# Sums of x1's halves on VectorE, and the low half of a half tile behind the next addition: a hybrid decoder layer on one core

## The chip, the cores and the metric

One core of a Trainium2 chip. The metric is device microseconds of one execution of the whole layer; less is better. The kernel before takes 2071.34 us (median of three runs, 2071.24 to 2073.43).

## The reference

One decoder layer in float32 on 512 tokens of width 2048. A token mixer (a gated recurrence and differential attention) and its output projection come first; then a residual and a layer norm; then a gated MLP of width 5632 with a causal convolution of width 3 behind the up-projection; then a residual and a second layer norm. Cut to the part that matters here:

```python
mix = jnp.einsum('bsm,md->bsd', jnp.concatenate([rg_out, at_out], axis=-1), w_out[i])
x = _layernorm(DEEPNORM_ALPHA * x + mix, ln_mix_g[i], ln_mix_b[i])
hu = _causal_dwconv(jnp.einsum('bsd,df->bsf', x, w_up[i]), ffn_conv_w[i], ffn_conv_b[i])
g, u = jnp.split(hu, 2, axis=-1)
ffn = jnp.einsum('bsf,fd->bsd', jax.nn.gelu(g) * u, w_down[i])
```

The x of the second line is called x1 here.

## The kernel before

Every matmul is made of several in a rounded format: a value is split into a high half (ScalarE copies it, rounded, L113) and a low half (VectorE subtracts the high half from the value, L114), and a product takes high x high, high x low and low x high (`mm3`, L120). So a matrix operand is ready for TensorE only when ScalarE and then VectorE have been over it.

Tokens are cut into 4 tiles of 128 (`QB`), the width of 2048 into 16 tiles of 128 (`KT`) or 4 blocks of 512 (`NF`). The stages around the change are these.

**The norms.** The last part of the output projection runs over 4 token tiles and, in each, over 4 blocks `fb` (L722 to L735). For each block TensorE makes six matmuls, VectorE adds them onto y and sums the row (`RowNorm.add`, L585), and ScalarE squares the result with its row sum (L592). Behind the four blocks come the mean (L597 to L600), the variance and its root (L604 to L608) and, in `norm_z`, the scaling of y: block 0 on ScalarE (L711), block 1 on VectorE, the others on GpSimd, except that block 2 of the last token tile is VectorE's too (L714). Each scaled block is stored (L715).

**x1, turned.** `turn_x1` (L666) makes half a tile of x1 with the width on the partitions and 256 tokens along the row: TensorE transposes two blocks (L672), ScalarE scales and shifts them into `x1f` (L682) and copies the high half, VectorE makes the low half (`split`, L684). There are 32 such half tiles, in the order of the list `first`; the first seven hold only tokens of the first two token tiles, which are scaled already while the last token tile is added up. Three of them (`LEAD`) are turned ahead, in the last token tile before blocks 1, 2 and 3 (L725). After that the loop at L739 turns half tile i + 3 and then multiplies half tile i with weights into four sums (`up_first`, L686, 12 matmuls each).

All this, from L721 to L742, is under `tc.manual_schedule()`: each engine gets its instructions in the order in which they are written. Behind that section, a planner orders each engine's instructions by their priority (the place in the program) and by the times at which its own model takes their inputs to be ready. Each engine then works through its queue in that order.

**Two plain blocks.** The results of the first two up-projections are activated (`activate`, four `tap`s on ScalarE, L778, convolutions on VectorE, L772). Then two more blocks of the up-projection run plainly (the loop `for i in range(2, PLAIN)`), in eight units of 48 matmuls. After each unit `forms(j)` (L749) makes the operands of the stage after: of x1f[j] and x1f[j + 8], each in two halves of 256 tokens, four sums are formed (L755 to L758, on GpSimd) into two temporary tiles from a ring of 12, and each sum is split into a high and a low half (L764, L765 and the helper's L113, L114). The weights of each unit are split as well (`wlo<-raw,whi` is their low half).

**The stage after.** 40 blocks of the up-projection use seven products of half size each in place of eight, on the operands that `forms` made. For these, GpSimd's queue issues DMAs that add one block of weights onto another in place (`onto`, L804).

Of the kernel before, what the change touches and what calls it, by code (L numbers as in the profile page):

```python
# [12 lines left out]
AF = mybir.ActivationFunctionType  # L13
ALU = mybir.AluOpType
# [10 lines left out]
QB = S // P  # L25
# [35 lines left out]
LEAD = 3  # L61
# [13 lines left out]
def f32(ap):  # L75
    return ap.bitcast(F32)
# [3 lines left out]
def trunk_kernel(  # L80
    ctx, tc, xT, x_tok, w_qkg, w_v, gate_w, w_out, w_up0, w_up, w_down, ln1, ln2, consts, out
):
    nc = tc.nc
# [10 lines left out]
    def bank():  # L94
        return psum.tile([P, S], F32, tag="ps", bufs=8, name="ps")

    def a_tile(dt=F32R, name="a"):
        return act.tile([P, S], dt, tag="a", bufs=A_BUFS, name=name)

    def t_tile(dt=F32, name="t"):  # L100
        return tmp.tile([P, S], dt, tag="t", bufs=T_BUFS, name=name)

    def c_tile(name):
        return W.pool.tile([P, 2 * S], F32, tag="c", bufs=4, name=name)
# [4 lines left out]
    def split(src, hi=None, lo=None, mk=a_tile):  # L109

        hi = mk(F32R, "hi") if hi is None else hi
        lo = mk(F32R, "lo") if lo is None else lo
        nc.scalar.activation(hi, src, AF.Copy)  # L113
        nc.vector.tensor_tensor(lo, src, f32(hi), ALU.subtract)  # L114
        return hi, lo

    def mm3(ps, w, x, first, last, onto=False):

        for n, (a, b) in enumerate(((w[0], x[0]), (w[0], x[1]), (w[1], x[0]))):
            nc.tensor.matmul(  # L120
                ps, a, b, start=first and n == 0, stop=last and n == 2, skip_group_check=onto
            )
# [85 lines left out]
    def col(i, n=1):  # L208
        return cst[:, i : i + n]
# [410 lines left out]
    def token(tt):  # L620
        return slice(tt * P, (tt + 1) * P)

    for fb in range(NF):
# [7 lines left out]
        for u in range(UO):  # L631
# [7 lines left out]
            for n in range(2):  # L639
                i = 2 * u + n  # L640
# [7 lines left out]
        for tt in range(QB):  # L648
            y = ys[tt, fb] = a_tile(F32, "y")
# [4 lines left out]
    x1 = [[None, None] for _ in range(KT)]  # L654
# [5 lines left out]
    def sides(z):  # L660
        return z[:, :HALF], z[:, HALF:]

    def split2(z):
        return z[:, :S], z[:, S:]

    def turn_x1(n, h):  # L666

        kt, tok = ks[n], halves[h]
        pt = bank()[:, :HALF]
        for i in range(2):  # L670
            c = slice(kt % 4 * P, (kt % 4 + 1) * P)
            nc.tensor.transpose(pt[:, i * P : (i + 1) * P], ys[2 * h + i, kt // 4][:, c], ident)  # L672
        if h == 0:
            j = kt % (KT // 2)
            if j < 4:

                if kt == j:
                    x1f[kt], x1f[kt + KT // 2] = split2(c_tile("x1f"))
            else:
                x1f[kt] = a_tile(F32, "x1f")  # L680
        y = x1f[kt][:, tok]
        nc.scalar.activation(y, pt, AF.Identity, scale=col(C_G1 + kt), bias=col(C_B1 + kt))  # L682
        x1[kt][h] = a_tile(F32R, "x1")
        split(y, *sides(x1[kt][h]))  # L684

    def up_first(n, h):  # L686
        kt, tok = ks[n], halves[h]
        if wu[n] is None:
            wu[n : n + 2] = W.take()
        hi, lo = wu[n]  # L690
        for t in range(4):
            c = slice(t * P, (t + 1) * P)
            mm3(
                pu[t][:, tok], (hi[:, c], lo[:, c]), sides(x1[kt][h]),
                n + h == 0, n == KT - 1 and h == 1,
            )

    first = [
        (n - h * AHEAD, h) for n in range(KT + AHEAD) for h in range(2) if n - h * AHEAD in range(KT)
    ]  # L700
    def norm_root(tt):
        norms[tt].var()

    def norm_z(tt):

        nmean, r = norms[tt].nmean, norms[tt].rstd()
        nc.vector.tensor_tensor(norms[tt].d2, nmean, r, ALU.mult)
        for fb in range(NF):
            y = ys[tt, fb]
            if fb == 0:  # L710
                nc.scalar.activation(y, y, AF.Identity, scale=r, bias=norms[tt].d2)  # L711
            else:
                eng = nc.vector if fb == 1 or (fb == 2 and tt == QB - 1) else nc.gpsimd
                eng.tensor_scalar(y, y, nmean, r, ALU.add, ALU.mult)  # L714
            nc.sync.dma_start(x1d[tt][:, fb * S : (fb + 1) * S], y)  # L715
# [5 lines left out]
    with tc.manual_schedule():  # L721
        for tt in range(QB):  # L722
            norms.append(RowNorm())
            for fb in range(NF):
                if tt == QB - 1 and 0 < fb <= LEAD:  # L725
                    turn_x1(*first[fb - 1])
                ps = bank()
                for n in range(2):
                    hs = [z[:, token(tt)] for z in ms[2 * UO + n]]
                    mm3(ps, hs, wl[fb][n], n == 0, n == 1)  # L730
                norms[tt].add(fb, ys[tt, fb], ps)

                if tt and fb < 2:
                    (norm_root, norm_z)[fb](tt - 1)
            norms[tt].mean()  # L735
        norm_root(QB - 1)
        norm_z(QB - 1)
        pu = [bank() for _ in range(4)]
        for i, at in enumerate(first):  # L739
            if i + LEAD < len(first):  # L740
                turn_x1(*first[i + LEAD])
            up_first(*at)  # L742


# [3 lines left out]

    def forms(j):  # L749
        a, b = x1f[j], x1f[j + KT // 2]  # L750
        sub = nc.gpsimd.tensor_tensor
        t14, t23 = t_tile(F32, "t14"), t_tile(F32, "t23")
        (t1, t4), (t2, t3) = sides(t14), sides(t23)
        (b11, b12), (b21, b22) = sides(a), sides(b)
        sub(t1, b12, b11, ALU.subtract)  # L755
        sub(t2, t1, b22, ALU.subtract)
        sub(t4, t2, b21, ALU.add)
        sub(t3, b22, b12, ALU.subtract)  # L758
        form["p1", j], form["p2", j] = x1[j][0], x1[j + KT // 2][0]
        form["p3", j] = x1[j + KT // 2][1]  # L760
        for name, t in (("p5", t1), ("p4", t4)):
            z = form[name, j] = a_tile(F32R, "hl")
            hi, lo = sides(z)
            nc.scalar.activation(hi, t, AF.Copy, scale=-1.0)  # L764
            nc.vector.scalar_tensor_tensor(lo, t, -1.0, f32(hi), ALU.mult, ALU.subtract)  # L765
        for name, t in (("p6", t2), ("p7", t3)):
            form[name, j] = a_tile(F32R, "hl")
            split(t, *sides(form[name, j]))
# [147 lines left out]
    for i in range(2, PLAIN):  # L916
        pss = []
        for g in range(2):
            ps = bank()
            for half in range(2):  # L920
                parts = W.take()
                left = 4 * (PLAIN - i) - 2 * g - half
                if left <= 6:
                    step(-left, "before", -6, 5)
                for kk in range(8):
                    kt = half * 8 + kk
                    hi, lo = parts[kk // 4]
                    c = slice((kk % 4) * P, (kk % 4 + 1) * P)
                    for h, tok in enumerate(halves):
                        mm3(  # L930
                            ps[:, tok], (hi[:, c], lo[:, c]), sides(x1[kt][h]),
                            kt + h == 0, kt == KT - 1 and h == 1,
                        )
                forms(j)
                j += 1
            pss.append(ps)
        activate(i, pss)
# [36 lines left out]
    for c, n in enumerate(CHUNKS[:-1]):  # L974
        ready(at + n)
        for fb in range(NF):
            ps = [bank() for _ in range(QB)]
            if c == 0:
# [4 lines left out]
                for tt in range(QB):  # L983
                    y = acc[tt, fb] = a_tile(F32, "acc")
# [14 lines left out]
            for tt in range(QB):  # L999
                y = acc[tt, fb]  # L1000
# [102 lines left out]
def build(arrays):  # L1103
    import concourse.bacc as bacc

    nc = bacc.Bacc("TRN2", target_bir_lowering=False, num_devices=1)
    args = [
        nc.dram_tensor(f"in_{n}", arrays[n].shape, F32, kind="ExternalInput").ap() for n in _INS
    ]
    args.append(nc.dram_tensor("out", (S, D), F32, kind="ExternalOutput").ap())  # L1110
    with tile.TileContext(nc) as tc:
        trunk_kernel(tc, *args)
    return nc
# [10 lines left out]
```

## Time and profile before

| | |
|---|---|
| median of the runs | 2071.34 us (2071.24 to 2073.43) |
| the profiled execution, its own time | 2071.46 us |
| its span, from the first instruction to the last | 2069.6 us |
| TensorE busy | 2043.6 us (99%) |
| VectorE busy | 1377.7 us (67%) |
| ScalarE busy | 1038.2 us (50%) |
| GpSimd busy | 135.0 us (7%) |
| mean granted clock of TensorE | 0.995 of full speed |

A busy TensorE says little of what limits it, since its matmuls follow each other closely all the way. What counts is where it is not busy, what ended each such wait, and where its clock was granted at half. In rows, PE is TensorE, PEld its weight load, DVE VectorE, ACT ScalarE, POOL GpSimd. Times are in us from the start of the span; a row of the timeline may hold several instructions in succession (x2).

### The profile page before, as it was taken

The numbers are of one execution on the slowest core, as the hardware profiler recorded it, in microseconds if no ns is written. First come the engines' busy times: TensorE is split into PE (matmuls) and PEld (weight loads), VectorE is DVE, ScalarE is ACT, GpSimd is POOL, SyncE is SP. The second block draws the span as 40 slices with busy tenths as digits, with TensorE's granted clock in tenths as the row PEclk, the third lists the DMA queues.
The fourth block names the chain that finished last, engine by engine and source line by source line (L and its number), as shares of the span: only waits on it lengthen the run. The fifth ranks groups of instructions, "written<-read, shape, count | busy, mean of one in ns | idle before, by whom it ended". The sixth has DMA issues, their size and how long they took to land.

```text
span 2069.6 us, 27751 instructions
## 1 busy us (share of the span) xinstructions
PE 2043.6 (99%) x10535; PEld 1749.7 (85%) x10535; DVE 1377.7 (67%) x2116; ACT 1038.2 (50%) x1652; POOL 135.0 (7%) x193
## 2 busy tenths in 40 slices
PE   9999999999999989999999999999999999999997
PEld 7888888888888889888888888888888888888886
DVE  6566645778335587888888888888889643333346
ACT  5475735668223745565566566565566232222232
POOL 1000000000000150001000000100000000000000
PEclk9999999999999999999999999999999999999999
DMA  6223222223522425576676676676678843243322
GB/s 221 97 72 97 75 96 79 87 82 113 183 92 102 157 73 128 158 191 171 166 190 173 164 187 178 164 185 176 169 182 272 278 138 117 92 142 92 112 82 82
DMA packets 93157, 290.53 MB, mean 140 GB/s; under 512 B 10336, under 2 KB 10336, under 8 KB 93024
## 3 DMA queue, kind: packets, MB, share of 16 engines
q1 hardware_dynamic: 81504, 246.81, 35.7%
q0 software_dynamic: 11520, 41.95, 11.8%
q8 instruction: 83, 1.36, 0.3%
q14 instruction: 50, 0.41, 0.1%
HBM read 268.80 MB, written 19.92 MB: 140 GB/s over the span
## 4 chain that ended last, share of the span: by engine, by line
PE 94%; ACT 3%; DVE 2%; issue 0%; DMA 0%; DVEq 0%
PE ps L120 55%; PE ps L134 37%; DVE x L114 1%; PE ps L364 1%; ACT gt L473 0%; PE ps L365 0%; ACT s L376 0%; PE ps L394 0%; PE ps L672 0%; ACT a L479 0%; ACT L491 0%; ACT L479 0%; ACT L473 0%; ACT L376 0%; DVE hh L495 0%
## 5 line engine op out<-in xcount | busy, mean ns | idle before, releaser
L114 DVE TENSOR_TENSOR wlo<-raw,whi 128x512 fp32r<-128x512 f32 (+1 forms) x672 | 601.2, 913 | 421.4 <-ACT whi L113 420.1
L113 ACT ACTIVATE whi<-raw 128x512 fp32r<-128x512 f32 (+1 forms) x672 | 522.6, 802 | 471.8 <-PE ps L120 412.1
L120 PE MATMUL ps<-wlo,hi 128*128 128x512 f32 x992 | 386.3, 389 | 0.6 <-DVE wlo L114 0.6
L120 PE MATMUL ps<-whi,hi 128*128 128x512 f32 x992 | 385.9, 389 | 0.4 <-ACT hi L113 0.4
L120 PE MATMUL ps<-whi,lo 128*128 128x512 f32 x992 | 385.8, 389 | 0.0
L134 PE MATMUL ps<-hl,whi 128*128 128x512 f32 x1280 | 320.5, 392 | 0.0
L134 PEld LDWEIGHTS ps<-hl,whi 128*128 128x128 f32 x1280 | 230.2, 189 | 41.1
L134 PE MATMUL ps<-x,whi 128*128 128x512 f32 x960 | 237.1, 389 | 0.0
L120 PEld LDWEIGHTS ps<-wlo,hi 128*128 128x128 f32 x992 | 186.3, 188 | 39.7 <-DVE wlo L114 1.2
L120 PEld LDWEIGHTS ps<-whi,hi 128*128 128x128 f32 x992 | 186.3, 188 | 39.6 <-ACT hi L113 1.1
L120 PEld LDWEIGHTS ps<-whi,lo 128*128 128x128 f32 x992 | 186.2, 188 | 38.9 <-DVE lo L114 0.2
L134 PEld LDWEIGHTS ps<-x,whi 128*128 128x128 f32 x960 | 180.2, 188 | 37.3
L120 PE MATMUL ps<-hi,whi 128*128 128x512 f32 x512 | 201.8, 394 | 0.0
L120 PE MATMUL ps<-hi,wlo 128*128 128x512 f32 x512 | 200.5, 392 | 1.2 <-DVE wlo L114 1.2
L120 PE MATMUL ps<-lo,whi 128*128 128x512 f32 x512 | 200.0, 391 | 0.0
L134 PE MATMUL ps<-hl,wlo 128*128 128x256 f32 x1280 | 173.0, 283 | 0.0
L134 PEld LDWEIGHTS ps<-hl,wlo 128*128 128x128 f32 x1280 | 164.6, 192 | 3.5 <-ACT cu L875 0.4
L134 PEld LDWEIGHTS ps<-x,wlo 128*128 128x128 f32 x960 | 131.0, 190 | 9.3
L134 PE MATMUL ps<-x,wlo 128*128 128x256 f32 x960 | 133.9, 282 | 0.0
L804 POOL DMA_DIRECT2D raw<-in_w_up x80 | 69.4, 871 | 759.1 <-DVE raw L824 427.4
L120 PEld LDWEIGHTS ps<-hi,wlo 128*128 128x128 f32 x512 | 96.1, 188 | 22.6 <-DVE wlo L114 2.4
L120 PEld LDWEIGHTS ps<-lo,whi 128*128 128x128 f32 x512 | 96.3, 188 | 18.5
(187 smaller groups left out, 2302.8 us busy)
## 6 DMA issues: line engine op xcount, KB each, us to landing
raw<-in_w_up SPq DMA_DIRECT2D x176, 512.0 KB, 5.2
raw<-in_w_down SPq DMA_DIRECT2D x88, 512.0 KB, 3.5
raw<-in_w_up POOLq DMA_DIRECT2D x80, 512.0 KB, 7.1
raw<-in_w_qkg SPq DMA_DIRECT2D x64, 512.0 KB, 3.6
raw<-in_w_out SPq DMA_DIRECT2D x32, 512.0 KB, 3.5
hidd<-cv SPq DMA_DIRECT2D x44, 256.0 KB, 3.9
hid<-hidd SPq DMA_DIRECT2D x44, 256.0 KB, 5.1
raw<-in_w_v SPq DMA_DIRECT2D x15, 512.0 KB, 4.2
```

The costliest lines, as they stand in the source:

```text
L113: nc.scalar.activation(hi, src, AF.Copy)
L114: nc.vector.tensor_tensor(lo, src, f32(hi), ALU.subtract)
L120: nc.tensor.matmul(ps, a, b, start=first and n == 0, stop=last and n == 2, skip_group_check=onto)
L134: nc.tensor.matmul(o, a, b, start=not onto and k == 0, stop=k == len(steps) - 1, skip_group_check=onto)
L364: nc.tensor.matmul(ps[:, :L], qs, k[c][:, :L], start=True, stop=False)
L804: nc.gpsimd.dma_start(self.raw[name], w_up[2 * (self.i - 2) + g][:, n * 1024 : (n + 1) * 1024], accum_op=ALU.add,)
```

## The change

In `turn_x1` the call of `split` is written out. The high half is issued as before; the low half is returned as a function, to be called by the caller. In the loop of the norms, it is called behind the addition of the block ahead of which the half tile was turned; in the loop at L739 it is called at once, as before. In `forms`, the four sums are issued on VectorE in place of GpSimd.

```diff
@@ turn_x1
         y = x1f[kt][:, tok]
         nc.scalar.activation(y, pt, AF.Identity, scale=col(C_G1 + kt), bias=col(C_B1 + kt))
         x1[kt][h] = a_tile(F32R, "x1")
-        split(y, *sides(x1[kt][h]))
+        hi, lo = sides(x1[kt][h])
+        nc.scalar.activation(hi, y, AF.Copy)
+
+        return lambda: nc.vector.tensor_tensor(lo, y, f32(hi), ALU.subtract)
@@ the loop of the norms
             for fb in range(NF):
-                if tt == QB - 1 and 0 < fb <= LEAD:
-                    turn_x1(*first[fb - 1])
+                ahead = tt == QB - 1 and 0 < fb <= LEAD
+                if ahead:
+                    rest = turn_x1(*first[fb - 1])
                 ps = bank()
                 for n in range(2):
                     hs = [z[:, token(tt)] for z in ms[2 * UO + n]]
                     mm3(ps, hs, wl[fb][n], n == 0, n == 1)
                 norms[tt].add(fb, ys[tt, fb], ps)
+                if ahead:
+                    rest()
@@ the loop of the first up-projection
             if i + LEAD < len(first):
-                turn_x1(*first[i + LEAD])
+                turn_x1(*first[i + LEAD])()
             up_first(*at)
@@ forms
         a, b = x1f[j], x1f[j + KT // 2]
-        sub = nc.gpsimd.tensor_tensor
+        sub = nc.vector.tensor_tensor
```

## Rows read from the trace of the kernel before

**Rows 1.** Waits of TensorE, whole run: us in total, times, longest.
```profile
PE ps L120 <- DVE x L114: 7.9, 1, 7.9
PE ps L120 <- ACT x L113: 2.5, 1, 2.5
...
PE ps L672 <- DVE total L585: 0.9, 1, 0.9
```
**Rows 2.** Timeline of VectorE, 734 to 748: start, length, instruction, idle time before and releaser.
```profile
734.64 0.42 DVE L114 TENSOR_TENSOR x<-x1f,x 128x256 fp32r<-128x256 f32 x1 [1.21 <-ACT x L113]
736.30 11.73 DVE L114 TENSOR_TENSOR x<-x1f,x 128x256 fp32r<-128x256 f32 x2 [1.24 <-ACT x L113]
```
**Rows 3.** Timeline of GpSimd, 735 to 760; fourteen like sums are left out.
```profile
735.41 1.03 POOL L804 DMA_DIRECT2D raw<-in_w_up  x1 [42.73 <-DMA raw<-in_w_up]
736.23 1.00 POOL L755 TENSOR_TENSOR t<-x1f 128x256 f32<-128x256 f32 x1
...
746.51 0.90 POOL L757 TENSOR_TENSOR t<-t,x1f 128x256 f32<-128x256 f32 x1
759.07 0.79 POOL L755 TENSOR_TENSOR t<-x1f 128x256 f32<-128x256 f32 x1 [11.67 <-DMA hidd<-cv]
```
**Rows 4.** Busy time by stretches: length, each engine (instructions), clock, DMA share, GB/s.
```profile
694.95:698.35 3.40, 3.40 (x18) 3.40 (x17) 1.78 (x4) 3.17 (x7) 0.00 (x0) 0.51 1.08 271
747.75:752.82 5.07, 5.07 (x23) 5.07 (x24) 1.15 (x3) 1.68 (x3) 0.00 (x0) 0.50 0.00 0
752.82:798.99 46.17, 46.17 (x386) 46.17 (x386) 39.80 (x61) 24.35 (x54) 16.76 (x18) 1.00 0.31 84
```
**Rows 5.** Timeline of VectorE at the end of the norms.
```profile
682.35 0.42 DVE L114 TENSOR_TENSOR x<-x1f,x 128x256 fp32r<-128x256 f32 x1 [1.77 <-ACT x L113]
682.69 0.68 DVE L585 CUSTOM_DVE_ANT_0 y<-y,ps 128x512 f32<-128x512 f32 x1
...
689.03 0.68 DVE L585 CUSTOM_DVE_ANT_0 y<-y,ps 128x512 f32<-128x512 f32 x1
...
690.79 0.16 DVE L605 SCALAR_TENSOR_TENSOR r<-r,d 128x1 f32<-128x1 f32 x1
```
**Rows 6.** Timeline of ScalarE in the same stretch.
```profile
681.90 0.42 ACT L113 ACTIVATE x<-x1f 128x256 fp32r<-128x256 f32 x1
683.41 0.73 ACT L592 ACTIVATE sq<-y,nshift 128x512 f32<-128x512 f32 x1 [1.10 <-DVE total L585]
...
684.14 0.80 ACT L711 ACTIVATE y<-y,d,r 128x512 f32<-128x512 f32 x1
684.84 0.55 ACT L682 ACTIVATE x1f<-ps,cst 128x256 f32<-128x256 f32 x1
```
**Rows 7.** Timeline of TensorE in the same stretch.
```profile
680.83 0.38 PE L672 MATMUL ps<-ident,y 128*128 128x128 f32 x2
...
684.17 0.48 PE L120 MATMUL ps<-x,hi 128*128 128x256 f32 x2
...
693.47 0.85 PE L120 MATMUL ps<-x,hi 128*128 128x256 f32 x2 [2.51 <-ACT x L113]
```
**Rows 8.** VectorE's groups by form, 757 to 776: count, busy us, mean ns, idle before.
```profile
L765 DVE SCALAR_TENSOR_TENSOR hl<-t,hl 128x256 fp32r<-128x256 f32 x8 | 7.0, 890 | 0.0
L114 DVE TENSOR_TENSOR hl<-t,hl 128x256 fp32r<-128x256 f32 x8 | 5.7, 752 | 0.0
L114 DVE TENSOR_TENSOR wlo<-raw,whi 128x512 fp32r<-128x512 f32 x4 | 4.7, 1225 | 0.0
```
**Rows 9.** The same groups, 776 to 800.
```profile
L114 DVE TENSOR_TENSOR wlo<-raw,whi 128x512 fp32r<-128x512 f32 x6 | 3.9, 683 | 1.3 <-ACT whi L113 1.3
...
L765 DVE SCALAR_TENSOR_TENSOR hl<-t,hl 128x256 fp32r<-128x256 f32 x8 | 3.2, 417 | 0.0
```
**Rows 10.** Timeline of ScalarE behind the section that is ordered by hand.
```profile
751.14 2.79 ACT L778 ACTIVATE cv<-ps,cst 128x512 f32<-128x512 f32 x4 [13.24 <-PE ps L120]
753.81 0.43 ACT L764 ACTIVATE hl<-t 128x256 fp32r<-128x256 f32 x1
```

## The prediction

> **What bounds the kernel now.** TensorE is busy for 99% of the span, so the first view to read is the list of what TensorE waited for. It is short. One wait of 7.9 us on VectorE's low half of x1 and one of 2.5 us on ScalarE's high half are nearly all of it; a third, of 0.9 us, is on the addition of a row norm [rows 1]. Both large ones lie where the change works, so a gain is to be had there and only there; elsewhere time is TensorE's own work, which the change leaves alone.
>
> The second view is VectorE's order of time around the 7.9 us. A subtraction of 128x256 that takes 0.42 us just before, and its successor, fill 11.73 us from 736.30 to 748.03 [rows 2]; taking the successor's 0.42 and its 0.08 of overlap off, the first alone has some 11.4. GpSimd starts its first sum at 736.23, and sixteen follow each other without a gap, the last from 746.51 to 747.41 [rows 3]. The subtraction ends just after that. VectorE is not working in this time, it is kept out while GpSimd's sums run, and TensorE needs what it makes.
>
> The third view is the granted clock by stretches. For 5.07 us after the long wait TensorE has 0.50 of full speed, 1.2 in place of 2.4 GHz, and for 3.40 us after the shorter one 0.51 [rows 4]. So each wait has a second price behind it.
>
> The fourth is the norms' end, VectorE and ScalarE side by side [rows 5, 6]. Each of the three low halves that are turned ahead holds VectorE for about 1.77 us, since ScalarE has not written the high half yet; the next block's addition stands behind it. ScalarE in turn has the square of that addition next, ahead of the next half's copies. The two engines wait for each other in a ring, three times round, and TensorE resumes only at 693.47 [rows 7].
>
> **Part one: the sums go to VectorE.** Removed from GpSimd: 32 sums of 128x256 (four for each of eight j). Added to VectorE: the same 32.
> The wait: VectorE's last two low halves no longer meet GpSimd's sums. In steady state a low half stands some three steps ahead of its use, so TensorE goes on through its last 24 matmuls. Removed: 7.9 us. These 24 take 5.07 us at 1.2 GHz [rows 4]; at 2.4 GHz 386 take the 46.17 us of the next stage, 0.12 each [rows 4], so 24 take 2.9. Removed: 2.2 us more. Sum of part one on the path: 10.1 us.
> The added work: a low half of the same shape frees VectorE 0.34 us after its start (682.35 to 682.69, [rows 5]), so 32 sums take 10.9 us. They lie in the stage after x1, where TensorE works 46.17 us on two up-projection blocks and VectorE is busy 39.80 of them [rows 4]. But the contention goes as well. While the second sixteen sums ran on GpSimd, VectorE's conversions took 890 and 752 ns, and the low halves of weights 1225; later in the same stage they take 417 and 683 [rows 8, 9]. The excess is 8 x 0.47 + 8 x 0.34 + 4 x 0.54 = 8.6 us. VectorE then has 39.8 - 8.6 + 10.9 = 42.1 us to do in 46.2: it fits, with 4.1 us to spare, and TensorE covers it. I cost the added sums at nothing. If that cover is gone, they cost between 0 and the 8.7 us of the second rival.
> Where they will stand: on ScalarE the first conversion of a sum, at 753.81, stands behind four taps which wait for the end of the block, though its sum was done before 738 [rows 3, 10]. The planner thus took the sums to be ready only about when the block ends, so on VectorE I put them behind the last low half, not ahead of it. GpSimd's queue keeps its DMAs alone, and these no longer have sums before or behind them.
>
> The Trainium skill, "SBUF — State Buffer", in its part on how VectorE and GpSimd share a port pair, says that a VectorE instruction with two SBUF inputs and a GpSimd instruction that reads SBUF lock each other out for a whole instruction. The trace agrees that one is kept out, and shows more: sixteen sums in a row went by before the subtraction had its turn [rows 2, 3]. A rule speaks against the change: "VectorE: DVE Perf Modes", section "The DRAIN you can't avoid", has the next instruction start only when the pipe is empty. By that, each sum would cost its full 0.42 us, 13.4 in all, and VectorE would have 44.6 of 46.2 us; the rows show 0.34 from start to start, and the sum goes by these.
>
> **Part two: the low half behind the addition.** Nothing is added; three subtractions trade places with three additions on VectorE, and no DMA is moved past anything. The first addition concerned could start as soon as its matmuls are done, before 681.3 (TensorE has gone on to the next transposes at 680.83 [rows 7]), in place of 682.69. Then ScalarE is the chain. Its first high half starts at 681.90 and takes 0.4: 682.3. The square follows at once, 0.7: 683.0. The scaling of y, 0.7: 683.7, or 683.8 with its wait for the mean. Then x1f 0.6, high half 0.4, square 0.7, x1f 0.6: the third high half starts at 686.1 (durations from [rows 6]). Its low half starts 0.45 later, as 682.35 stands to 681.90, and frees VectorE at 686.9. The statistics behind it took 690.79 - 689.03 - 0.68 = 1.1 us up to their last product [rows 5]; that comes at about 687.9 in place of 690.79. All that follows up to TensorE's restart is as before, so TensorE resumes at about 690.6 in place of 693.47. Sum of part two: 2.9 us. What is late next: TensorE begins the block's first up-projection at 684.17 and needs three of them with their transposes, 1.6 us each (12 matmuls at 0.12 and a pair of transposes), and is at the fourth at 689.1. It then still waits about 1.5 us, now on ScalarE's work.
> The clock behind that wait: at 1.2 GHz a matmul takes 5.07 / 24 = 0.21 us for 0.12, so 3.40 us there hold 1.5 us of extra time [rows 4]. In this trace the 2.5 us wait was followed by the lower clock, and the 0.9 us one not within 5 us of it. A wait of 1.5 lies between them; 0 and 1.5 us are the ends, and I take half, 0.7.
>
> **Sum.** 10.1 + 2.9 + 0.7 = 13.7 us. The profiled execution's own time is 2071.46 us (span 2069.6), 0.12 above the median. 2071.46 - 13.7 = 2057.8, and against the median 2057.6.
>
> **The rivals.**
> First, the contention is not the sums' but that of GpSimd's accumulating DMA, which is issued just ahead of them. Then part of the stall stays. For it: both stand in the same queue at the same moment. Against it: the subtraction ends with the last sum, and in the later stretch VectorE is slow again where sums run and no such DMA does. If half of part one stays, 5 us, the time is 2062.7. Chance 0.05.
> Second, VectorE becomes late in the two-block stage: the sums stand ahead of a weight's low half that TensorE needs. All 32 ahead of it make it 10.9 us later, less some half of the contention, 4.3: 6.5 us of wait, and 2.2 of lower clock behind it as above, 8.7 in all, if there is no slack. For it: VectorE would be 91% busy. Against: TensorE had no wait there before, with VectorE slowed by 8.6 us. From no loss to 8.7, the middle is 2062. Chance 0.17.
> Third, part two gives nothing, since ScalarE alone sets the ring: 2060.5. For it: ScalarE has little idle time in those 10 us. Against: its waits for VectorE's additions are part of the ring. Chance 0.06.
> Fourth, the change doesn't do what it says: the planner places sixteen sums ahead of the last two low halves on VectorE, so they hold them 16 x 0.34 = 5.4 us in place of 11.4. TensorE had 11.4 - 7.9 = 3.5 us of lead, so it waits 1.9 and perhaps 2.2 for the clock: 2059.5 to 2061.7. Chance 0.05.
> Fifth, slower. The later sums need a temporary buffer; on GpSimd the first of them waited 11.67 us for the store of an activated tile [rows 3], and nothing was behind it. On VectorE's in-order queue such a hold stops the weights' low halves. VectorE has 4.1 us to spare, so a hold of 11.67 makes TensorE wait 7.6 and 2.2 for the clock: 2067.4, still faster. It is slower than before from a hold of 4.1 + 13.7 - 2.2 = 15.6 us on; two such holds, 23.3 us, give 19.2 + 2.2 - 13.7 = 7.7 us more than before, 2079. Against: most of the 11.67 us was TensorE's wait and the taps, which come before the sums in the order expected here. Chance 0.05.
>
> **How the numbers follow.** The forecast, both waits gone or shortened as worked out, has 0.62: 2057.6, or 2056.9 to 2058.3 by the clock. If TensorE's remaining 1.5 us went too, it would be 2055.4, which is the low end. The high end takes in the second rival up to about four fifths of its price, 2064.6. Outside lie the slower case and the ends of the others. A measurement of this kernel can tell about 0.2%, 4.1 us, from no change. Faster by more than that holds in the forecast and in most of all rivals but the fifth: 0.90. Within 0.2%: 0.05. Slower: 0.05.
>
> **What would show each step.** Right for part one: no VectorE subtraction on x1 over 1 us long, TensorE without a wait at the block's end, the clock at 1.00 there, no sums on GpSimd, and conversions at 0.42 us throughout. Right for part two: no idle time of VectorE ahead of the three additions, TensorE's wait on the high half at 1 to 2 us, resuming some 3 us earlier counted from the first transpose. Wrong would be: a new wait of TensorE on a weight's low half in the two-block stage (second or fifth rival), a long subtraction with GpSimd idle (first), or a low half late behind sums (fourth).

## The result, and the profile after

The changed kernel takes 2057.03 us, the median of three runs (2056.8 to 2058.12), where the kernel before takes 2071.34. The ratio is 0.9929, with a 95% interval of 0.9907 to 0.9952: 14.3 us less, between 10 and 19. In a second series, with five runs and nine of the kernel before, the ratio was 0.9934 [0.9921, 0.9946] and the median 2056.33. Forecast were 2057.6 us.

The profiled execution of after took 2058.12 us, its span is 2055.9. First, what TensorE still waits for (us in total, times, longest):

```profile
PE ps L120 <- DVE wlo L114: 1.8, 5, 0.6
PE ps L292 <- DVE warm L289: 1.5, 1, 1.5
PE ps L120 <- ACT x L685: 0.9, 1, 0.9
```

The first two stand in the kernel before as well, in other stages and as long; the prediction's list, which called 0.9 us the third, passes over them. Of the three waits of [rows 1] the 7.9 us on VectorE's low half is gone, the 2.5 us on ScalarE's high half has become 0.9, and the 0.9 us on the addition is gone.

The busy time of three stretches: the one behind the 0.9 us wait, the end of x1's block, and the two-block stage (length, then PE, PEld, DVE, ACT, POOL, clock, DMA share, GB/s):

```profile
694.95:698.35 3.40, 3.40 (x31) 3.40 (x31) 2.51 (x5) 3.23 (x7) 0.00 (x0) 1.00 1.01 279
734.50:739.65 5.15, 5.15 (x45) 5.15 (x44) 0.49 (x2) 1.47 (x4) 0.00 (x0) 1.00 0.53 94
739.65:785.82 46.17, 46.17 (x387) 46.17 (x386) 42.39 (x94) 26.33 (x56) 1.73 (x2) 1.00 0.35 98
```

In [rows 4] the first two kinds of stretch had a clock of 0.51 and 0.50. Here it is 1.00 in all three: TensorE does 31 matmuls in 3.40 us where it did 18, and 45 in 5.15 where it did 23 in 5.07. The two-block stage takes the same 46.17 us as before, with VectorE busy for 42.39 of them in place of 39.80.

TensorE at three points: the first transposes ahead of the norm blocks, its restart behind the remaining wait, and the first matmul of the two-block stage (start, length, instruction, idle time before):

```profile
681.13 0.38 PE L672 MATMUL ps<-ident,y 128*128 128x128 f32 x2
...
692.20 0.85 PE L120 MATMUL ps<-x,hi 128*128 128x256 f32 x2 [0.93 <-ACT x L685]
...
739.65 0.40 PE L120 MATMUL ps<-x,whi 128*128 128x256 f32 x2
```

From the first point to the last are 58.52 us; this length is called the block's below. Before it was 73.60, since the stage began at 752.82 [rows 4] and the transposes at 679.22:

```profile
679.22 0.38 PE L672 MATMUL ps<-ident,y 128*128 128x128 f32 x2
```

So the block lost 15.08 us. The rest of this execution gives 1.7 back, since its block began 1.91 us later, behind the same instructions in the same order on every engine. In the profiles here this start lies anywhere from 679.1 to 681.1, and so the length of the block is a sharper measure than the whole time. In the profile of the second series the block began at 679.36 and took 58.52 again, and that execution took 2056.33 us, 15.1 less than the 2071.46 of before.

VectorE in the same time: the end of the norms, the end of the block, the sums behind it.

```profile
682.94 0.69 DVE L585 CUSTOM_DVE_ANT_0 y<-y,ps 128x512 f32<-128x512 f32 x1 [0.45 <-PE ps L120]
684.26 0.42 DVE L687 TENSOR_TENSOR x<-x1f,x 128x256 fp32r<-128x256 f32 x1 [0.63 <-ACT x L685]
685.33 0.68 DVE L585 CUSTOM_DVE_ANT_0 y<-y,ps 128x512 f32<-128x512 f32 x1
...
688.35 0.43 DVE L687 TENSOR_TENSOR x<-x1f,x 128x256 fp32r<-128x256 f32 x1 [0.58 <-ACT x L685]
689.52 0.16 DVE L605 SCALAR_TENSOR_TENSOR r<-r,d 128x1 f32<-128x1 f32 x1
...
733.49 0.42 DVE L687 TENSOR_TENSOR x<-x1f,x 128x256 fp32r<-128x256 f32 x1 [1.22 <-ACT x L685]
735.16 0.43 DVE L687 TENSOR_TENSOR x<-x1f,x 128x256 fp32r<-128x256 f32 x1 [1.24 <-ACT x L685]
...
745.62 0.41 DVE L761 TENSOR_TENSOR t<-x1f 128x256 f32<-128x256 f32 x1
...
750.58 0.68 DVE L114 TENSOR_TENSOR wlo<-raw,whi 128x512 fp32r<-128x512 f32 x1
```

The last two low halves of x1 take 0.42 and 0.43 us each, where they filled 11.73 in [rows 2]. The additions at L585 now come ahead of the low halves. The first of the three still has 0.45 us of idle time ahead of it, in which it waits for TensorE's matmuls, where the prediction's sign was none at all; the other two have none. The first sum stands at 745.62, some 10 us behind the last low half of x1.

VectorE's groups by form in the two-block stage, 739.65 to 785.82 (count, busy us, mean ns of one, idle before):

```profile
L114 DVE TENSOR_TENSOR wlo<-raw,whi 128x512 fp32r<-128x512 f32 x10 | 6.7, 682 | 0.0
L771 DVE SCALAR_TENSOR_TENSOR hl<-t,hl 128x256 fp32r<-128x256 f32 x16 | 6.6, 416 | 0.0
L114 DVE TENSOR_TENSOR hl<-t,hl 128x256 fp32r<-128x256 f32 x16 | 6.2, 417 | 0.1
L761 DVE TENSOR_TENSOR t<-x1f 128x256 f32<-128x256 f32 x8 | 3.3, 417 | 0.0
```

The means are 682, 416 and 417 ns for the whole stage: what [rows 9] had only behind the sums, and not the 1225, 890 and 752 of [rows 8].

### The profile page after: what moved, and what is told of

It is laid out like the page before. It is cut to its first block, busy times and chain, and to the rows that moved or that the text cites. A ratio compares the mean times of both kernels' runs of the same rounds, so it can differ in the third digit from the quotient of the medians.

```text
span 2055.9 us, 27746 instructions
## 1 busy us (share of the span) xinstructions
PE 2040.5 (99%) x10535; PEld 1747.2 (85%) x10535; DVE 1369.0 (67%) x2148; ACT 1039.2 (51%) x1652; POOL 108.8 (5%) x161
## 4 chain that ended last, share of the span: by engine, by line
PE 94%; ACT 3%; DVE 1%; issue 0%; DMA 0%; SPq 0%; DVEq 0%
PE ps L120 55%; PE ps L134 37%; PE ps L364 1%; ACT gt L473 0%; PE ps L365 0%; ACT s L376 0%; PE ps L394 0%; PE ps L672 0%; ACT a L479 0%; DMA hid<-hidd 0%; ACT L491 0%; ACT L479 0%; ACT L473 0%; ACT L376 0%; DVE hh L495 0%
## 5 line engine op out<-in xcount | busy, mean ns | idle before, releaser
L120 PEld LDWEIGHTS ps<-hi,whi 128*128 128x128 f32 x512 | 96.2, 188 | 18.3
```

The costliest lines, as they stand in the source:

```text
L120: nc.tensor.matmul(ps, a, b, start=first and n == 0, stop=last and n == 2, skip_group_check=onto)
```

## The experiments

**Part one alone.** In the kernel before, only the sums' engine is changed.

```
-        sub = nc.gpsimd.tensor_tensor
+        sub = nc.vector.tensor_tensor
```

> Part one alone: the 32 sums on VectorE, the three low halves ahead of the additions as in the kernel before. If the two parts add up as the prediction has it, the wait of 7.9 us on the low half and the half clock behind it go (10.1 us), and the ring of VectorE and ScalarE with its 2.5 us wait and its 3.4 us of half clock stays: 2061.2 us. If the whole gain of 14.3 us is the sums' and the order of the low halves is of no account: 2057. If the sums only pay together with part two (VectorE too late in the two-block stage without it): above 2063, with a wait of TensorE on a weight's low half.

Measured: 2060.97 us, ratio 0.9957 [0.9944, 0.9969] against 2070.32 for the kernel before on the same chip, 9.35 us less. The block takes 63.00 us, 10.60 less. TensorE's waits, and the stretch behind the larger one:

```profile
PE ps L120 <- ACT x L113: 2.5, 1, 2.5
PE ps L672 <- DVE total L585: 0.9, 1, 0.9
...
693.70:697.50 3.80, 3.71 (x17) 3.54 (x18) 1.70 (x4) 2.75 (x8) 0.00 (x0) 0.55 1.03 302
```

The 7.9 us wait is gone, the two of the norms' end stay to the tenth, and so does the half clock behind the first of them. The parts thus act at different places.

**Part two alone.** The changed kernel with the sums back on GpSimd.

```
-        sub = nc.vector.tensor_tensor
+        sub = nc.gpsimd.tensor_tensor
```

> Part two alone: the three low halves behind the additions, the sums on GpSimd as in the kernel before. If the parts add up: the 2.5 us wait shrinks to 0.9 to 1.5 us, TensorE resumes some 3 us earlier after it without the half clock (1.5 us), and the wait of 7.9 us on a low half stays with its half clock: 2066.9 us. If the order is of no account: 2071.3. If TensorE, being earlier at the end of the block, only waits there longer for the same sums: 2071 too, but with a wait of over 10 us in place of 7.9.

Measured: 2067.85 us (2065.92 to 2068.91), ratio 0.9986 [0.9978, 0.9995], 2.5 us less. TensorE behind the two waits, and two stretches behind the second:

```profile
690.71 0.84 PE L120 MATMUL ps<-x,hi 128*128 128x256 f32 x2 [0.91 <-ACT x L685]
...
744.01 0.58 PE L120 MATMUL ps<-x,hi 128*128 128x256 f32 x1 [7.01 <-DVE x L687]
744.01:746.52 2.51, 2.51 (x12) 2.51 (x12) 0.87 (x2) 1.68 (x3) 0.00 (x0) 0.50 0.00 0
746.52:749.40 2.88, 2.88 (x15) 2.88 (x15) 2.88 (x5) 2.85 (x5) 0.00 (x0) 0.52 0.00 0
```

The first wait is 0.91, as in the changed kernel (0.93), and TensorE resumes 11.05 us behind its first transposes, which began at 679.66, in place of 14.25. The second wait is still there, 7.01 us, and now the 1.2 GHz reach 2.88 us into the next stage: 15 matmuls there against the 24 that 2.88 us hold at 0.12 each, so some 1.1 us of the block's gain are lost behind it. The block is 66.86 us, 6.74 less; what is left of that, about 5.6, is more than the 2.5 us of the medians. The profiled execution was one of the quicker ones, 2066.23 us or 5.2 under that of before; single runs of this kernel spread over 3 us. So part two's worth by itself is known only to lie between about 1 and 5.5 us. The two parts' gains add up to 11.8 by the medians and to 16.2 by the blocks; both together gave 14.0 to 14.3 and 15.08. So they add within what these numbers can tell, some 2 us either way: the medians' sum is below what both gave, the blocks' sum above it.

**Half as many sums in a row.** The first sixteen sums in a row are those of j = 0 to 3. Those of j = 0 and 1 go to VectorE, so that eight are left in the row. The order of low halves and additions is that of before.

```
-        sub = nc.gpsimd.tensor_tensor
+        sub = (nc.vector if j < 2 else nc.gpsimd).tensor_tensor
```

> The kernel before with the sums of j = 0 and 1 on VectorE and those of j = 2 to 7 on GpSimd, so that about eight sums (j = 2, 3) in place of sixteen can follow the DMA in GpSimd's queue. If VectorE's low half is held as long as the run of sums lasts, it is held 8 x 0.69 = 5.5 us in place of 11.4, TensorE has 3.5 us of lead and waits about 2 us: with no half clock behind it 2063.2, with it 2065.4. If it is the accumulating DMA ahead of the sums that holds it, the low half takes 11 us and the time stays at 2071.

Measured: 2064.19 us, ratio 0.9968 [0.9957, 0.9979], 6.1 less; the block 67.50, 6.10 less. VectorE's two low halves, what TensorE waited, and GpSimd's DMA with the first and the last of the eight sums:

```profile
736.18 6.37 DVE L114 TENSOR_TENSOR x<-x1f,x 128x256 fp32r<-128x256 f32 x2 [1.21 <-ACT x L113]
...
742.27 0.39 PE L120 MATMUL ps<-x,hi 128*128 128x256 f32 x1 [2.54 <-DVE x L114]
```

```profile
735.34 1.03 POOL L804 DMA_DIRECT2D raw<-in_w_up  x1 [42.76 <-DMA raw<-in_w_up]
736.16 0.99 POOL L755 TENSOR_TENSOR t<-x1f 128x256 f32<-128x256 f32 x1
...
741.00 0.91 POOL L757 TENSOR_TENSOR t<-t,x1f 128x256 f32<-128x256 f32 x1
```

By the working used on [rows 2], the first low half alone has 6.37 - 0.34 = 6.0 us and ends at 742.2, just behind the last sum. TensorE's wait on it is 2.5 us. With sixteen sums the two numbers were 11.4 and 7.9. The difference is 3.5 us both times: that is TensorE's lead, and what goes beyond it is paid in full. The wait follows the length of the run of sums, while the DMA ahead of it is the same. The lower clock follows this shorter wait too: the 24 matmuls behind it take 4.35 us, up to 746.62, where 2.9 would do at 2.4 GHz. So the case with half clock is the one that came, and its 2065.4 lies 1.2 us above the median.

**GpSimd writes, and reads nothing.** The sums are left out; GpSimd fills their targets with zeros in their place and order.

```
-        sub = nc.gpsimd.tensor_tensor
+        def sub(o, *_):
+            nc.gpsimd.memset(o, 0.0)
```

> The kernel before, with each of the 32 sums on GpSimd replaced by a fill of the same half tile with zero: the operands of four of the seven products are left out, so the output is not the reference's. GpSimd then writes the same bytes and reads nothing. If it is GpSimd's reading that keeps out a VectorE subtraction with two inputs, the low halves stay at 0.42 us while the fills run, and the 7.9 us wait is gone: about 2061. If writing is enough, the low half is held for as long as the sixteen fills last, some 16 x 0.2 to 0.5 us = 3 to 8 us, and TensorE waits 0 to 5 us.

Measured, in one run: 2062.38 us; the block takes 64.27, 9.33 less. VectorE's last two low halves, and GpSimd's DMA and fills:

```profile
737.94 0.42 DVE L114 TENSOR_TENSOR x<-x1f,x 128x256 fp32r<-128x256 f32 x1 [1.23 <-ACT x L113]
739.59 0.42 DVE L114 TENSOR_TENSOR x<-x1f,x 128x256 fp32r<-128x256 f32 x1 [1.22 <-ACT x L113]
```

```profile
737.26 1.03 POOL L806 DMA_DIRECT2D raw<-in_w_up  x1 [43.98 <-DMA raw<-in_w_up]
738.05 4.38 POOL L752 MEMSET t<- 128x256 f32 x16
```

Sixteen fills run from 738.05 to 742.43, and a low half in the middle of them takes its 0.42 us. The DMA is there, the row of sixteen instructions is there, and TensorE doesn't wait for the low half. So it is not the DMA, and not that GpSimd is busy. What the fills leave out is the reading of SBUF; but a fill is also shorter, 0.27 us in the row where a sum takes 0.69, and does no arithmetic. Its length hardly explains it, since a low half beside the fills isn't held at all. In the kernel before, fills of twice that length, of 64 partitions and at another place, leave a subtraction with two inputs in SBUF alone too, though the two overlap by 0.14 us only:

```profile
165.48 1.09 POOL L520 MEMSET k<- 64x512 f32 x2
166.43 0.69 DVE L114 TENSOR_TENSOR lo<-sq,hi 128x512 fp32r<-128x512 f32 x1 [0.75 <-ACT hi L113]
```

So the reading is the likeliest cause; that a sum computes as well was not varied alone. The block is 1.27 us longer than part one's, although the same wait is gone. That lies at the norms' end, where the 2.5 us wait had a longer stretch of half clock behind it in this execution than the 3.4 us of [rows 4]:

```profile
694.07:700.20 6.13, 6.13 (x27) 5.96 (x28) 3.03 (x7) 4.58 (x10) 0.00 (x0) 0.50 1.04 316
```

**The sums on GpSimd, but early.** In the kernel before, the four sums of j are written as soon as their halves are there, four at a time between the up-projections, for the first four j. `sums(j)` holds the four lines from `forms`, still on GpSimd, and `forms` then takes the results that are there.

```
             up_first(*at)
+            n, h = at
+            if h == 1 and n % 2 == 1 and n < 8:
+                sums(n // 2)
```

> The kernel before with the sums of j = 0 to 3 still on GpSimd, but written into the section that is ordered by hand, each j behind the up-projection of the half tile that completes it; so they stand ahead of the DMA in GpSimd's queue and run in fours, spread over the block. If what costs is that sixteen come in one run at the block's end, each four hold VectorE 4 x 0.69 = 2.8 us at most, less than TensorE's lead of 3.5, and the 7.9 us wait is gone with its half clock: 2061.2, as with the sums on VectorE. If any sum on GpSimd costs TensorE time, there are four waits in the block and the time lies between 2062 and 2071.

Measured: 2060.65 us, ratio 0.9954 [0.994, 0.9968], within 0.4 of part one alone; the block 63.04, against its 63.00. The 7.9 us wait is gone, the 2.5 and 0.9 stay. The longest low half of x1 among these sums:

```profile
706.60 0.97 DVE L114 TENSOR_TENSOR x<-x1f,x 128x256 fp32r<-128x256 f32 x1 [0.61 <-ACT x L113]
```

So the engine is not what costs, nor that sums and low halves meet. The four of a j don't even follow each other closely: the first of one j starts at 701.60, the others at 704.89, 705.79 and 706.55. Spread like this they hold a low half by half a microsecond at most, which TensorE's lead covers; sixteen without a gap hold it for more than the lead. What four without a gap would do was not run.

**Every sum twice on VectorE.** The changed kernel, with 64 sums in place of 32, to see what the added work costs when its cover is used up.

```
-        sub = nc.vector.tensor_tensor
+        def sub(*a):
+            nc.vector.tensor_tensor(*a)
+            nc.vector.tensor_tensor(*a)
```

> The changed kernel with each of the 32 sums issued twice on VectorE, so 10.9 us more of its work in the two-block stage. The prediction has VectorE at 42.1 of 46.2 us there. If that is right, 53 us no longer fit: TensorE waits at the end of the stage or for a weight's low half, 2 to 7 us and up to 2.2 us of half clock behind it: 2059 to 2066. If VectorE has more room than that (some of its work in the stage is not needed until later), the time stays at 2057.

Measured: 2062.73 us, ratio 0.996 [0.9945, 0.9975]: 6.4 us more than the changed kernel in the same series. The two-block stage and the time behind its end, and TensorE there:

```profile
738.45:784.62 46.17, 46.17 (x387) 46.17 (x386) 46.03 (x108) 22.94 (x46) 1.75 (x2) 1.00 0.24 67
794.06:799.40 5.34, 5.34 (x17) 4.62 (x18) 3.86 (x4) 0.00 (x0) 0.00 (x0) 0.52 0.40 125
...
794.06 2.04 PE L134 MATMUL ps<-hl,wlo 128*128 128x256 f32 x8 [3.74 <-DVE wlo L114]
```

VectorE is busy for 46.03 of the stage's 46.17 us, and what doesn't fit is late in the stage behind: TensorE waits 3.74 us there for a weight's low half and then runs at 1.2 GHz for nearly all of 5.34 us, in which 17 matmuls were done. The wait, and about half of the 5.34 us for the clock, make some 6.4 us. This is the second rival's mechanism, with its place moved one stage on. The added 32 x 0.34 = 10.9 us brought 3.7 us of wait, so by this estimate the changed kernel had about 7.2 us to spare: 46.17 - 42.39 = 3.8 in the stage, the rest in the one behind, where VectorE isn't full.

**A fourth half tile turned ahead.** The changed kernel with LEAD = 4, the fourth half tile turned ahead of the last row norm's scaling, against the 0.9 us wait that remains.

```
-LEAD = 3
+LEAD = 4
...
-                ahead = tt == QB - 1 and 0 < fb <= LEAD
+                ahead = tt == QB - 1 and 0 < fb < LEAD
...
+        rest = turn_x1(*first[LEAD - 1])
         norm_root(QB - 1)
+        rest()
         norm_z(QB - 1)
```

> The changed kernel with a fourth half tile turned ahead: its transposes, copies and low half stand ahead of the last token tile's root and scaling. In the changed kernel TensorE still waits 0.9 us for the high half of that tile, since ScalarE scales y first. If that is all that is late there, the wait goes and the time is 0.9 to 1.2 us lower than the changed kernel's: 2055.9. If the scaling, being later by 0.3 to 0.9 us, is what TensorE then waits for, nothing is gained: 2057.

Measured: 2055.79 us, ratio 0.9933 [0.992, 0.9945]. The block takes 57.89 us, 0.63 less than the changed kernel's. The one wait that TensorE has in it now:

```profile
695.67 0.39 PE L120 MATMUL ps<-x,lo 128*128 128x256 f32 x1 [0.22 <-DVE lo L114]
```

The 0.9 us wait is gone, and the clock stays at 1.00. The 0.22 us are another wait, some 5 us further on than that one was, for the low half of a weight. Less is gained than the 0.9 us that were expected at least, and that the whole is faster than the changed kernel is not shown: the run of the latter in the same series follows, and the two differ by 0.5 us where the single runs of each spread over 2.6 to 2.7.

**The changed kernel in the same series,** unchanged, as the measure for the two runs above.

> The changed kernel once more, on the same chip as the three above, so that they can be compared with it: 2057.0 us.

Measured: 2056.33 us (2056.22 to 2058.92), ratio 0.9934 [0.9921, 0.9946].

## Why the prediction was right, point by point

**The long wait.** Right in cause and size. The subtraction was kept out by the run of GpSimd's sums: eight in place of sixteen shortened its hold from 11.4 to 6.0 us, with fills, which read nothing, a low half took 0.42. Part one on the path was put at 10.1 us; alone it gave 10.60 in the block and 9.35 in the medians. In the changed kernel, what is left of the block's 15.08 us without part two's 3.2 and 1.5 (below) is 10.4. The clock behind the wait was a fifth of that term and came as worked out: [rows 4] had 0.50 where after has 1.00.

**The added sums at nothing.** Right. Forecast were 42.1 us of VectorE's work in the two-block stage, and 42.39 were measured: the contention's 8.6 us did go, and TensorE has no new wait there. A sum costs 0.34 us. That is plainest where the kernel with doubled sums has them in a row on VectorE:

```profile
784.38 0.41 DVE L758 TENSOR_TENSOR t<-t,x1f 128x256 f32<-128x256 f32 x1
784.72 0.41 DVE L758 TENSOR_TENSOR t<-x1f 128x256 f32<-128x256 f32 x1
785.05 0.41 DVE L759 TENSOR_TENSOR t<-t,x1f 128x256 f32<-128x256 f32 x1
```

Each is recorded with 0.41 us and starts 0.34 behind the last. The Trainium skill, "VectorE: DVE Perf Modes", section "The DRAIN you can't avoid", has the next instruction wait for an empty pipe, but adds that one which is not held starts earlier, which the prediction left out; the trace agrees with the addition, and the 44.6 us that the first half of the rule would have given did not come. What the prediction called 4.1 us of spare time was 3.8 in the stage, and there was more of it behind the stage than was counted.

**Where the sums stand.** Right: behind the last low half of x1 and behind the first convolutions of the stage, the first at 745.62. Neither the fourth rival nor the fifth came; no VectorE instruction is held by a store, and the weights' low halves keep 682 ns.

**Part two.** Right in mechanism, with two terms mis-sized, both to the same side. With the 1.91 us by which this block began later taken off, the third low half starts at 686.44, where it was put at 686.1 plus 0.45; the last product of the statistics at 687.61, where 687.9 was forecast for 690.79 [rows 5]; and TensorE resumes at 690.29 for 690.6, in place of 693.47 [rows 7]. That is 3.18 us for 2.9. TensorE reached the wait at 689.36, where 689.1 was worked out, so that 0.93 us were left and not about 1.5. The other term: the lower clock behind the wait was costed at half of 1.5 us, and there was none. TensorE ran at 1.00 in the same stretch where it had 0.51, so the whole 1.5 came back. No wait of 0.91 to 0.93 us here had the lower clock behind it; what a wait of the forecast 1.5 us would have had, no run shows, and half was a guess between two ends.

**The sum.** 13.7 us were forecast. With part one as its own run had it, the same terms measured are 10.6 + 3.2 + 1.5 = 15.3, and the block of the changed kernel lost 15.08. The medians show 14.3 and 14.0. The error of 0.6 us against the median is smaller than what single runs spread by, so it is the terms that test the working, not the sum. That the forecast lies closer to the medians than the sum of its measured terms does is luck.

**The other rivals.** The accumulating DMA (first) is out: it stands ahead of the fills and ahead of the eight sums alike, and with the fills no low half is held, with the eight sums only until they end. VectorE late (second) did not come at this size, but does from some 7 us more work. That part two gives nothing (third) is out by 11.05 us in place of 14.25 with part two alone. That rival's 2060.5 took off only the 2.9 us; with the 0.7 us for the clock gone as well it is 2061.2, and part one alone measured 2060.97.

## What to carry to other kernels

A wait of the busiest engine on an instruction that is far longer than its likes is worth a look at what another engine starts and ends at the same times: here the cost was not the other engine's work but sixteen instructions of it in a row, and either moving them to the engine they held up, or spreading them out, ended it. When work is moved to the engine that was slowed by it, count the slowdown that goes (8.6 us) against the work that comes (10.9 us), and then measure the spare time once by doubling the addition. A wait's price is its length and what the lower clock takes behind it, and shortening a wait may return the second in full before the first is gone.

## What the runs showed of the hardware

**A row of instructions can keep another engine out as a whole.** The Trainium skill, "SBUF — State Buffer", in its part on the shared port pair, speaks of a lock for one instruction. That would let the subtraction in after 0.7 us, the step from one sum to the next; the traces show 11.4 us for sixteen sums and 6.0 for eight. In part two alone the subtraction comes 1.2 us behind the first of sixteen sums, which run from 732.47 to 743.66, and is kept out until the last:

```profile
733.65 10.30 DVE L687 TENSOR_TENSOR x<-x1f,x 128x256 fp32r<-128x256 f32 x1 [0.86 <-ACT x L685]
```

There is a reverse of it, in the kernel with early sums, where GpSimd's first sum behind the block meets VectorE's conversions:

```profile
742.13 2.86 POOL L728 TENSOR_TENSOR t<-x1f 128x256 f32<-128x256 f32 x1 [4.05 <-DVE hl L776]
744.95 0.74 POOL L731 TENSOR_TENSOR t<-x1f 128x256 f32<-128x256 f32 x1
```

```profile
741.95 0.76 DVE L114 TENSOR_TENSOR hl<-t,hl 128x256 fp32r<-128x256 f32 x2
742.62 0.76 DVE L776 SCALAR_TENSOR_TENSOR hl<-t,hl 128x256 fp32r<-128x256 f32 x2
743.30 0.75 DVE L114 TENSOR_TENSOR hl<-t,hl 128x256 fp32r<-128x256 f32 x2
743.97 0.42 DVE L776 SCALAR_TENSOR_TENSOR hl<-t,hl 128x256 fp32r<-128x256 f32 x1
744.30 4.68 DVE L783 SCALAR_TENSOR_TENSOR cv<-ps,cst,cv 128x511 f32<-128x511 f32 x7
```

The sum takes 2.86 us while VectorE's conversions, with both inputs in SBUF, follow each other every 0.34 us, and ends 0.7 us after VectorE has gone on to convolutions that take one input from PSUM. Beside those the next sums run at 0.74 us, undisturbed. The Trainium skill, "SBUF — State Buffer", in its part on who interferes with whom, says that an instruction of VectorE with at most one input in SBUF, outside certain modes that take both ports, doesn't contend with GpSimd, and that one with two inputs in SBUF contends with a GpSimd instruction that reads SBUF but not with one that only writes it. These rows agree, and so do the 0.42 us beside the fills.

**It is not always so.** In the stretch of [rows 8] conversions and sums went by turns: the conversions took 752 and 890 ns in the mean, and the sums started every 0.88 us, as one lock per instruction would have it. What decides between turns and keeping out was not settled.

**The clock.** In all five profiles with the 2.5 us wait at the norms' end TensorE ran at 1.2 GHz behind it, for some 3.5 us in four of them and for 6.1 in the fifth. Behind the waits of 0.91 to 0.93 us at the same place, in four profiles, it kept its 2.4 GHz.
